# A two-layer hybrid trunk: low weight parts last in the feed-forward products, one product accumulated onto a copy in PSUM, forgetting attention in one visit per block

## The chip, the cores and the metric

The kernel runs on one core of a Trainium2 chip. The core has a matrix engine (TensorE, PE), which reads its stationary operand by separate weight loads (PEld in the profile), a vector engine (VectorE, DVE), a scalar engine (ScalarE, ACT), GpSimd (POOL) and SyncE (SP), which here only starts DMA transfers. Each engine works through its own list of instructions; semaphores tie the lists together. The metric is the device time of one execution in microseconds. Times below are from the profile of one execution unless they are called a median.

## The reference

Two layers over x of 512 x 1024 (float32). In each layer three head groups share one projection w_in: sliding-window attention (group A), forgetting attention (group B) and mLSTM (group C).

```python
h = _rms(x, norm1)
z = h @ w_in
...
x = x + jnp.concatenate([ya, yb, yc], axis=-1) @ w_out
u = _rms(x, norm2) @ w_ff1
return x + jnp.square(jax.nn.relu(u)) @ w_ff2
```

Group B, in blocks of 128 queries, is a causal softmax with a decay taken from cumulated log gates:

```python
s = jnp.einsum('bqhd,bkhd->bhqk', qi, k).astype(jnp.float32) / math.sqrt(D)
s = s + Fi[..., None] - FT[:, :, None, :]
...
p = jax.nn.softmax(s, axis=-1).astype(v.dtype)
return jnp.einsum('bhqk,bkhd->bqhd', p, v)
```

## The kernel before, in words

x lies transposed in SBUF (xT, eight tiles of 128 rows by 512 columns). Every weight arrives in tiles of 128 x 1024 float32 (512 KB). For each, ACT copies a rounded high part (`whi`, L203) and DVE subtracts it from the raw tile to get the low part (`wlo`, L204). There are three buffers of each, so the parts of three jobs exist at a time. A product of weights and activations is then three matmuls: high by high, high by low, low by high (`mm3`, L261 to L263).

Raw tiles lie in a ring of three (`raw0` to `raw2`), to which the feed-forward phase adds a ring of four (`fraw`). `load_part` issues the plain load on SP's queue (L156); where a tile is the sum of two blocks, the second block is added to it by an accumulating transfer issued on POOL's queue (L158). A load is issued when a tile of a ring has been given back, that is when its `whi` and `wlo` are made.

In the feed-forward phase (about 246 to 538 us and 776 to 1068 us of the span) two rounds of w1 go by the plain scheme. The other six, and w2, go by a scheme of seven products on 2 x 2 blocks in place of eight, in the order A11, S1, S2, A12, S4, S3, A22. Two of the seven weights are made on DVE from tiles that are there already: `prep_job` adds S1's tile into A11's for S2 (L214), and A12's into that for S4 (L218). S1 and S3 are sums that the accumulating transfer makes. So the addition at L214 needs two things: that A11's `whi` and `wlo` have been made, and that S1's accumulating transfer has landed.

`prod` runs one such product: 4 k-slices x 2 halves x 3 matmuls of 256 columns, 24 in all. `ff_pairs` interleaves them, one product of w2 (`ff2`), one of w1 (`ff1_st`). A round of 14 products is seven of each. After each product `acc` (L1265) adds the result into xT, or `ff1_st` copies, adds, takes relu and square (`act`), and splits the activations into high and low parts (`gsplit`, L1167 and L1168; `csplit`, L1172 and L1173). The order of each engine's list is not the order of the code: the framework's scheduler moves instructions of one engine past one another where the data allow it, so an edit in one place can move instructions elsewhere.

All eight PSUM banks (`at`) hand round between products. In `ff1_st` the first product's result X is copied to SBUF (`ct[:, 0]`, ACT), the A12 product goes to a fresh bank Y, and DVE adds the two (L1233).

In the attention phase a generator `big_work` yields pieces of the w_in and w_out products; `fill(us, stop)` pulls pieces until a credit is used up, so that PE has dense work between the small matmuls of the groups. `runB` makes blocks in three steps: `s1` (scores at L849, mask at L851, then maximum, exponential, scaling on DVE and ACT), `s2` (transposes at L874, copies) and `s3` (values, L891). Step i runs `s1(i)` and `s3(i-2)`, yields, runs `s2(i-1)`, and yields again. Its generator is advanced by the loops over group C, with `fill` between the visits.

Of the kernel before, what the change touches and what calls it, by code (L numbers as in the profile page):

```python
# [15 lines left out]
AF = mybir.ActivationFunctionType  # L16
ALU = mybir.AluOpType
AX = mybir.AxisListType

P = 128  # L20
# [30 lines left out]
def trunk(ctx, tc, x, cols, rows, gate_w, tabs, w_in, w_out, w1, w2, out):  # L51
    nc = tc.nc
    V, A, G, T = nc.vector, nc.scalar, nc.gpsimd, nc.tensor
# [38 lines left out]
    def smt(n, name):  # L92
        return sm.tile([P, n], F32, tag=f"sm{n}", name=nm(name))

    def v3(a, d=HD):
        return a.rearrange("p (h d) -> p h d", d=d)
# [163 lines left out]
    def mm3(o, sh, sl, mh, ml, first, last, skip=False):  # L260
        T.matmul(o, sh, mh, start=first, stop=False, skip_group_check=skip)  # L261
        T.matmul(o, sh, ml, start=False, stop=False, skip_group_check=skip)  # L262
        T.matmul(o, sl, mh, start=False, stop=last, skip_group_check=skip)  # L263
# [132 lines left out]
    def headrms(zt, nh, name):  # L396
        sq = wt("tmp", "hsq")
        A.activation(sq[:, :nh * HD], zt, AF.Square)
        ss = smt(nh, name)
        V.tensor_reduce(ss, v3(sq[:, :nh * HD]), AX.X, ALU.add)  # L400
        v = smt(nh, name + "v")
# [39 lines left out]
    FA, FB = 2.1, 0.33  # L441
    F0, F1, F2 = 0, 4.5, 1.5
    FG = 4
    for l in range(L):
# [77 lines left out]
        done = set()  # L522
# [64 lines left out]
        bw = big_work()  # L587
        credit = [0.0]

        def fill(us, stop=None):  # L590
            credit[0] += us
            while credit[0] > 0:
                if stop is not None and stop in done:
                    credit[0] = 0.0
                    return
                c = next(bw, None)
                if c is None:
                    credit[0] = 0.0
                    return
                credit[0] -= c  # L600

        def fill_to(mark):
            while mark not in done:
# [130 lines left out]
        def runA():  # L734
# [7 lines left out]
            def s1(c):  # L742
# [8 lines left out]
                for r in range(2):  # L751
                    V.tensor_reduce(v3(mx, 2)[:, :, r], v3(sc[r], 256)[:, :, :nk], AX.X, ALU.max)
                nmx = smt(4, "nmx")
# [83 lines left out]
        def runB(qTB, kTB):  # L837
            units = [(pr, n) for pr in range(2) for n in range(NT)]
            st, pobs, fbs = {}, {}, {}

            def s1(u):
                pr, n = units[u]
                if n == 0:
                    fbs[pr] = [rowb(gate["drow"], 2 * pr + r) for r in range(2)]
                nk = (n + 1) * P
                sps = [att(), att()]
                for r, sp in enumerate(sps):
                    rs = slice(r * 64, (r + 1) * 64)
                    T.matmul(sp[:, :nk], qTB[rs, pr, n * P:(n + 1) * P], kTB[rs, pr, :nk], start=True, stop=False)  # L849
                for sp in sps:  # L850
                    T.matmul(sp[:, n * P:nk], identb, trib, start=False, stop=True)  # L851
                scs = [wt("scs", "scs") for _ in range(2)]
                mx, nmx, ssum, rec = (smt(2, n_) for n_ in ("mxb", "nmxb", "ssb", "recb"))
                for r, sp in enumerate(sps):
                    V.tensor_tensor_reduce(scs[r][:, :nk], sp[:, :nk], fbs[pr][r][:, :nk], 1.0, -3.0e38, ALU.add,
                                           ALU.max, mx[:, r:r + 1])
                V.tensor_scalar(nmx, mx, -1.0, None, ALU.mult)
                for r in range(2):
                    A.activation(scs[r][:, :nk], scs[r][:, :nk], AF.Exp, bias=nmx[:, r:r + 1],
                                 accum_out=ssum[:, r:r + 1])  # L860
                V.reciprocal(rec, ssum)
                for r in range(2):
                    V.tensor_scalar(scs[r][:, :nk], scs[r][:, :nk], rec[:, r:r + 1], None, ALU.mult)
                st[u] = scs

            def s2(u):
                pr, n = units[u]
                nk = (n + 1) * P
                scs = st.pop(u)
                ps = []  # L870
                for r in range(2):
                    pt = att()
                    for b in range(n + 1):
                        T.transpose(pt[:, b * P:(b + 1) * P], scs[r][:, b * P:(b + 1) * P], ident)  # L874
                    p_ = wt("pT", "pTb")
                    if r:
                        A.activation(p_[:, :nk], pt[:, :nk], AF.Copy)
                    else:
                        V.tensor_copy(p_[:, :nk], pt[:, :nk])
                    ps.append(p_)  # L880
                st[u] = ps

            def s3(u):
                pr, n = units[u]
                if n == 0:
                    pobs[pr] = att()
                ps = st.pop(u)
                for b in range(n + 1):
                    for r in range(2):
                        h = 2 * pr + r  # L890
                        T.matmul(pobs[pr][r * 64:(r + 1) * 64, n * P:(n + 1) * P], zbv[b][:, h * 64:(h + 1) * 64],  # L891
                                 ps[r][:, b * P:(b + 1) * P], start=b == 0, stop=b == n)
                if n == NT - 1:
                    A.activation(yhi(4 + pr), pobs[pr], AF.Copy)
                    V.tensor_tensor(ylo(4 + pr), pobs[pr], yhi(4 + pr), ALU.subtract)

            for i in range(len(units) + 2):
                if i < len(units):
                    s1(i)
                if 0 <= i - 2 < len(units):  # L900
                    s3(i - 2)
                yield
                if 0 <= i - 1 < len(units):
                    s2(i - 1)
                yield
# [126 lines left out]
        bt = 0  # L1032
# [31 lines left out]
        cst_ = wt("qk", "state")[:, :780].rearrange("p (b r v) -> p b r v", b=3, r=2)  # L1064
        G.memset(cst_, 0.0)
        for i in range(8):
            if i % 2 == 0:
                next(gb)
            fill(FB, "wo0")
            if i % 2 == 1:  # L1070
                prepC(i // 2, kTC)
                if i // 2 < NT - 1:
                    stateC(i // 2, cst_)
        gc, c_tail = runC(qTC, kTC, cst_)
        ct, bt = 0, 0
        for _ in gc:
            ct += 1
            fill(FB, "wo0")
            if 5 * bt < 2 * ct:
                bt += 1  # L1080
                next(gb, None)
                fill(FB, "wo0")
        for _ in gb:
            fill(FB, "wo0")
        fill_to("wo0")
        c_tail(0)
        fill_to("wo1")
# [7 lines left out]
        ct = v3(wt("ct", "ct"), S)  # L1095
# [11 lines left out]
        def bank():  # L1107
            return banks.popleft()
# [16 lines left out]

        def prod(bk, bh, bl, start):
            ws = getjob()
            for kk in range(4):
                hi, lo = ws[kk]
                for f in range(2):  # L1130
                    c = slice(f * P, (f + 1) * P)
                    mm3(bk[:, f * 256:(f + 1) * 256], hi[:, c], lo[:, c], bh(kk), bl(kk), start and kk == 0 and f == 0,
                        kk == 3 and f == 1, True)

        def prod1(bk, op, start=True):
            bh, bl = xop(op, 0), xop(op, 1)
            prod(bk, lambda kk: bh[:, kk, :], lambda kk: bl[:, kk, :], start)
# [37 lines left out]
        def act(a, src, sign):  # L1175
            A.activation(ct[:, a], src, AF.Relu, scale=sign)
            A.activation(ct[:, a], ct[:, a], AF.Square)
# [39 lines left out]
                    yield  # L1217

        def ff1_st(s, rr):
            X = bank()  # L1220
            prod1(X, 0)
            A.activation(ct[:, 0], X, AF.Copy)
            yield
            Z = bank()
            prod1(Z, 3)
            A.activation(ct[:, 3], Z, AF.Copy)
            yield
            prod1(X, 4, False)
            A.activation(ct[:, 1], X, AF.Copy)
            yield  # L1230
            Y = bank()
            prod1(Y, 1)
            V.tensor_tensor(ct[:, 0], Y, ct[:, 0], ALU.add)  # L1233
            banks.append(Y)
            act(0, ct[:, 0], 1.0)
            csplit(s, rr)
            yield
            prod1(Z, 2, False)
            V.tensor_tensor(ct[:, 1], Z, ct[:, 1], ALU.add)
            banks.append(Z)  # L1240
            act(1, ct[:, 1], 1.0)
            n1_()
            yield
            prod1(X, 5, False)
            V.tensor_tensor(ct[:, 3], X, ct[:, 3], ALU.add)
            act(3, ct[:, 3], -1.0)
            n2_(s, rr)
            yield
            prod1(X, 6, False)
            act(2, X, -1.0)  # L1250
            banks.append(X)
            tail_(s, rr)
            yield
# [23 lines left out]
        def ff2(s):  # L1277
# [18 lines left out]
            for dg in range(2):  # L1296
                Y = bank()
                prod2(Y, s, 1)
                acc(s, dg, 0, 0, Y, True)
                banks.append(Y)  # L1300
# [102 lines left out]
```

## Time and profile before

| | |
|---|---|
| median of three runs | 1079.09 us (1073.43 to 1081.91) |
| profiled execution: time, span | 1074.93 us, 1073.2 us |
| granted TensorE clock | 0.997 |
| PE busy, matmuls | 1059.1 us, 8376 |
| weight loads busy | 989.8 us |
| DVE busy | 911.9 us |
| ACT busy | 626.4 us |
| POOL busy | 103.8 us |

In the lists of waits a row names who waited for whom, then the total in us, the number of times and the longest. In timeline rows stand the start, the length, engine, line, operation, output and inputs, and in brackets how long the engine idled before and for what. In the chain of waits in order of time a row is a start, a length and what took it. "at<-xhl,whi" is a product into a PSUM bank of an activation tile and a high weight part; the activation tiles are called xhl, xbx, yg and gx. A start of a matmul is measured, its end is modelled, so distances are taken from start to start.

### The profile page before, as it was taken

The numbers are of one execution on the slowest core, as the hardware profiler recorded it, in microseconds if no ns is written. First come the engines' busy times: TensorE is split into PE (matmuls) and PEld (weight loads), VectorE is DVE, ScalarE is ACT, GpSimd is POOL, SyncE is SP. The second block draws the span as 40 slices with busy tenths as digits, with TensorE's granted clock in tenths as the row PEclk, the third lists the DMA queues.
The fourth block names the chain that finished last, engine by engine and source line by source line (L and its number), as shares of the span: only waits on it lengthen the run. The fifth ranks groups of instructions, "written<-read, shape, count | busy, mean of one in ns | idle before, by whom it ended". The sixth has DMA issues, their size and how long they took to land.

```text
span 1073.2 us, 20903 instructions
## 1 busy us (share of the span) xinstructions
PE 1059.1 (99%) x8376; PEld 989.8 (92%) x8376; DVE 911.9 (85%) x1550; ACT 626.4 (58%) x1097; POOL 103.8 (10%) x154
## 2 busy tenths in 40 slices
PE   8999999999999999999999999999999999999998
PEld 8999977887999999999999998778789999999998
DVE  6696877899997997988977878688999889799897
ACT  5446655376666566566454567444765665576662
POOL 2030020101010010010001200101000100000100
PEclk8999999999999999999999999999999999999999
DMA  6533121145478588588435321213334866876872
GB/s 200 164 110 109 59 68 50 62 174 118 118 197 215 140 213 209 149 210 223 108 108 155 102 80 41 86 44 136 112 87 141 233 178 172 219 183 191 211 185 99
DMA packets 47346, 151.81 MB, mean 141 GB/s; under 512 B 5632, under 2 KB 8832, under 8 KB 47248
## 3 DMA queue, kind: packets, MB, share of 16 engines
q1 hardware_dynamic: 39184, 121.10, 33.8%
q0 software_dynamic: 8064, 29.36, 16.2%
q8 instruction: 66, 1.08, 0.4%
q14 instruction: 32, 0.26, 0.1%
HBM read 147.86 MB, written 2.13 MB: 140 GB/s over the span
## 4 chain that ended last, share of the span: by engine, by line
PE 80%; DVE 11%; ACT 3%; DMA 3%; issue 1%; SPq 0%; DVEq 0%; POOLq 0%
PE at L261 24%; PE at L263 24%; PE at L262 24%; DMA raw<-in_w_dram 3%; DVE wlo L204 2%; DVE rt L719 2%; PE at L849 1%; PE at L891 1%; PE at L874 1%; ACT whi L203 1%; ACT pe L762 1%; PE at L972 1%; DVE yg L1168 1%; DVE z L715 1%; DVE z L721 1%
## 5 line engine op out<-in xcount | busy, mean ns | idle before, releaser
L203 ACT ACTIVATE whi<-raw 128x1024 fp32r<-128x1024 f32 (+1 forms) x144 | 150.9, 1048 | 143.7 <-PE at L262 103.2
L204 DVE TENSOR_TENSOR wlo<-raw,whi 128x1024 fp32r<-128x1024 f32 (+1 forms) x144 | 173.8, 1207 | 41.2 <-ACT whi L203 40.7
L203 ACT ACTIVATE whi<-fraw 128x1024 fp32r<-128x1024 f32 x122 | 129.2, 1060 | 92.4 <-PE at L262 76.2
L261 PE MATMUL at<-yg,whi 128*128 128x256 f32 (+1 forms) x592 | 179.8, 307 | 0.0
L263 PE MATMUL at<-yg,wlo 128*128 128x256 f32 (+1 forms) x592 | 178.4, 301 | 0.0
L262 PE MATMUL at<-xhl,whi 128*128 128x256 f32 (+1 forms) x576 | 177.9, 309 | 0.0
L262 PE MATMUL at<-yg,whi 128*128 128x256 f32 (+1 forms) x560 | 169.6, 303 | 0.0
L261 PE MATMUL at<-whi,xhl 128*128 128x256 f32 (+1 forms) x576 | 164.1, 285 | 2.1 <-ACT whi L203 1.3
L262 PE MATMUL at<-wlo,xhl 128*128 128x256 f32 (+1 forms) x576 | 161.5, 280 | 0.3 <-DVE wlo L204 0.3
L263 PE MATMUL at<-whi,xhl 128*128 128x256 f32 (+1 forms) x576 | 161.5, 280 | 0.0
L261 PE MATMUL at<-xhl,whi 128*128 128x256 f32 (+1 forms) x512 | 161.1, 315 | 0.0
L263 PE MATMUL at<-xhl,wlo 128*128 128x256 f32 (+1 forms) x512 | 160.3, 313 | 0.0
L204 DVE TENSOR_TENSOR wlo<-fraw,whi 128x1024 fp32r<-128x1024 f32 x122 | 148.9, 1221 | 8.6 <-ACT whi L203 8.1
L261 PEld LDWEIGHTS at<-yg,whi 128*128 128x128 f32 x592 | 111.2, 188 | 5.6 <-issue 1.7
L263 PEld LDWEIGHTS at<-yg,wlo 128*128 128x128 f32 x592 | 111.2, 188 | 5.3
L262 PEld LDWEIGHTS at<-xhl,whi 128*128 128x128 f32 x576 | 108.0, 188 | 7.6 <-issue 0.5
L261 PEld LDWEIGHTS at<-whi,xhl 128*128 128x128 f32 x576 | 109.4, 190 | 3.2 <-ACT whi L203 1.6
L262 PEld LDWEIGHTS at<-wlo,xhl 128*128 128x128 f32 x576 | 109.5, 190 | 0.5 <-DVE wlo L204 0.5
L263 PE MATMUL at<-xbx,wlo 128*128 128x256 f32 x384 | 106.6, 278 | 3.4 <-DVE wlo L204 3.4
L263 PEld LDWEIGHTS at<-whi,xhl 128*128 128x128 f32 x576 | 109.3, 190 | 0.3 <-DVE xhl L328 0.3
L262 PEld LDWEIGHTS at<-yg,whi 128*128 128x128 f32 x560 | 105.3, 188 | 4.2 <-DVE yg L1002 0.5
L261 PE MATMUL at<-xbx,whi 128*128 128x256 f32 x384 | 106.1, 276 | 0.0
(286 smaller groups left out, 2423.1 us busy)
## 6 DMA issues: line engine op xcount, KB each, us to landing
fraw<-in_w_dram SPq DMA_DIRECT2D x90, 512.0 KB, 4.5
raw<-in_w_dram SPq DMA_DIRECT2D x66, 512.0 KB, 4.5
raw<-in_w_in_dram SPq DMA_DIRECT2D x34, 512.0 KB, 3.4
fraw<-in_w_dram POOLq DMA_DIRECT2D x34, 512.0 KB, 6.0
raw<-in_w_dram POOLq DMA_DIRECT2D x22, 512.0 KB, 7.9
raw<-in_w_out_dram SPq DMA_DIRECT2D x16, 512.0 KB, 3.4
rowb<-drow SPq DMA_DIRECT2D x16, 256.0 KB, 4.0
raw<-in_w_in_dram SPq DMA_DIRECT2D x12, 256.0 KB, 3.8
```

The lines of the kernel that those rows point to most:

```text
L203: A.activation(hi[:, cs_], raw[:, cs_], AF.Copy)
L204: V.tensor_tensor(lo[:, cs_], raw[:, cs_], hi[:, cs_], ALU.subtract)
L261: T.matmul(o, sh, mh, start=first, stop=False, skip_group_check=skip)
L262: T.matmul(o, sh, ml, start=False, stop=False, skip_group_check=skip)
L263: T.matmul(o, sl, mh, start=False, stop=last, skip_group_check=skip)
L715: V.tensor_tensor(z10, z10, bc(rq), ALU.mult)
L719: V.tensor_tensor(r10[:, oo:oo + n, a:a + 32], z10[:, oo:oo + n, b:b + 32], tb(S_, n, a, a + 32), ALU.mult)
L721: V.tensor_tensor(zaq[t], ro[:, :640], rt[:, :640], ALU.add)
L762: A.activation(pe[:, u, :nk], sc[u % 2][:, (u // 2) * 256:(u // 2) * 256 + nk], AF.Exp, bias=nmx[:, u:u + 1], accum_out=ssum[:, u:u + 1])
L849: T.matmul(sp[:, :nk], qTB[rs, pr, n * P:(n + 1) * P], kTB[rs, pr, :nk], start=True, stop=False)
L874: T.transpose(pt[:, b * P:(b + 1) * P], scs[r][:, b * P:(b + 1) * P], ident)
L891: T.matmul(pobs[pr][r * 64:(r + 1) * 64, n * P:(n + 1) * P], zbv[b][:, h * 64:(h + 1) * 64], ps[r][:, b * P:(b + 1) * P], start=b == 0, st ...
```

## The change

Three edits. First, `prod` (the seven-product scheme alone) issues the sixteen matmuls with the high weight part for all k-slices and halves, and then the eight with the low part. Second, in `ff1_st` the first product's result is copied by ACT into a second PSUM bank Y, the A12 product accumulates onto it, and relu reads Y; the addition at L1233 is gone. Third, `runB` does one visit per block in place of two, the driving loops advance it half as often, and `fill` takes the w_out pieces in pairs.

```diff
-        def fill(us, stop=None):
+        def fill(us, stop=None, n=1):
             credit[0] += us
             while credit[0] > 0:
-                if stop is not None and stop in done:
...
-                credit[0] -= c
+                for _ in range(n):
...
+                    credit[0] -= c
...
                 if 0 <= i - 2 < len(units):
                     s3(i - 2)
-                yield
                 if 0 <= i - 1 < len(units):
                     s2(i - 1)
                 yield
...
         for i in range(8):
-            if i % 2 == 0:
+            if i % 4 == 0:
                 next(gb)
-            fill(FB, "wo0")
+            fill(FB, "wo0", 2)
...
-            if 5 * bt < 2 * ct:
+            if 5 * bt < ct:
                 bt += 1
                 next(gb, None)
-                fill(FB, "wo0")
+                fill(2 * FB, "wo0", 2)
         for _ in gb:
-            fill(FB, "wo0")
+            fill(2 * FB, "wo0", 2)
...
         def prod(bk, bh, bl, start):
             ws = getjob()
-            for kk in range(4):
-                hi, lo = ws[kk]
-                for f in range(2):
-                    c = slice(f * P, (f + 1) * P)
-                    mm3(bk[:, f * 256:(f + 1) * 256], hi[:, c], lo[:, c], bh(kk), bl(kk), start and kk == 0 and f == 0,
-                        kk == 3 and f == 1, True)
+            for i in range(2):
+                for kk in range(4):
+                    for f in range(2):
+                        c, o = slice(f * P, (f + 1) * P), bk[:, f * 256:(f + 1) * 256]
+                        w = ws[kk][i][:, c]
+                        T.matmul(o, w, bh(kk), start=start and i == kk == f == 0, stop=i == 1 and kk == 3,
+                                 skip_group_check=True)
+                        if i == 0:
+                            T.matmul(o, w, bl(kk), start=False, stop=False, skip_group_check=True)
...
         def ff1_st(s, rr):
-            X = bank()
+            X, Y = bank(), bank()
             prod1(X, 0)
-            A.activation(ct[:, 0], X, AF.Copy)
+            A.activation(Y, X, AF.Copy)
             yield
...
-            Y = bank()
-            prod1(Y, 1)
-            V.tensor_tensor(ct[:, 0], Y, ct[:, 0], ALU.add)
+            prod1(Y, 1, False)
+            act(0, Y, 1.0)
             banks.append(Y)
-            act(0, ct[:, 0], 1.0)
             csplit(s, rr)
```

What PE runs in one FF1 product of layer 0 (the one with weights whi_631 and wlo_632; xhl is the activation, at_ the bank), the last rows before the change:

```order
L261 MATMUL at_546_2966<-xhl_90,whi_631_4167 128x256
L262 MATMUL at_546_2966<-xhl_90,whi_631_4167 128x256
L263 MATMUL at_546_2966<-xhl_90,wlo_632_4168 128x256
L261 MATMUL at_546_2966<-xhl_90,whi_631_4167 128x256
L262 MATMUL at_546_2966<-xhl_90,whi_631_4167 128x256
L263 MATMUL at_546_2966<-xhl_90,wlo_632_4168 128x256
```

and the same product after it:

```order
L1133 MATMUL at_547_2967<-xhl_90,whi_631_4165 128x256
L1136 MATMUL at_547_2967<-xhl_90,whi_631_4165 128x256
L1133 MATMUL at_547_2967<-xhl_90,whi_631_4165 128x256
L1136 MATMUL at_547_2967<-xhl_90,whi_631_4165 128x256
L1133 MATMUL at_547_2967<-xhl_90,wlo_632_4166 128x256 x8
```

The low part wlo_632 stood third of each three and is now read by the last eight alone.

DVE's list at the same place (342.6 to 355 us of the span before): wlo_630 is the low part of an A11 tile of w2, raw1_74 that tile's raw weights, raw2_75 those of S1. Before:

```order
L204 TENSOR_TENSOR wlo_630_4138<-raw1_74,whi_629_4137 128x1024
L1183 SCALAR_TENSOR_TENSOR ct_527_2865<-ct_527_2865 128x512
L1184 TENSOR_TENSOR ct_527_2865<-ct_527_2865 128x512
L1265 TENSOR_TENSOR xT_89<-xT_89,at_544_2964 128x2x256
L204 TENSOR_TENSOR wlo_632_4168<-fraw_528_2866,whi_631_4167 128x1024
L1168 TENSOR_TENSOR gx_526_2864<-ct_527_2865,gx_526_2864 128x1024
L214 TENSOR_TENSOR fraw_528_2866<-fraw_528_2866 128x1024
L204 TENSOR_TENSOR wlo_634_4203<-fraw_528_2866,whi_633_4202 128x1024
L214 TENSOR_TENSOR raw1_74<-raw2_75,raw1_74 128x1024
L1168 TENSOR_TENSOR yg_91<-ct_527_2865,yg_91 128x1024
```

and after, where the lines of `ff1_st` and `acc` have moved by one to three (L1183 is L1186, L1184 is L1187, L1168 is L1171, L1265 is L1266):

```order
L204 TENSOR_TENSOR wlo_630_4136<-raw1_74,whi_629_4135 128x1024
L214 TENSOR_TENSOR raw1_74<-raw2_75,raw1_74 128x1024
L1186 SCALAR_TENSOR_TENSOR ct_527_2865<-ct_527_2865 128x512
L1187 TENSOR_TENSOR ct_527_2865<-ct_527_2865 128x512
L1266 TENSOR_TENSOR xT_89<-xT_89,at_545_2965 128x2x256
L1171 TENSOR_TENSOR gx_526_2864<-ct_527_2865,gx_526_2864 128x1024
L204 TENSOR_TENSOR wlo_632_4166<-fraw_528_2866,whi_631_4165 128x1024
L204 TENSOR_TENSOR wlo_634_4201<-fraw_528_2866,whi_633_4200 128x1024
L1171 TENSOR_TENSOR yg_91<-ct_527_2865,yg_91 128x1024
L1266 TENSOR_TENSOR xT_89<-xT_89,at_544_2964 128x2x256
```

The addition of S1's tile into A11's (L214 on raw1_74) has moved from eight instructions behind wlo_630 to the place directly behind it, ahead of wlo_632 and wlo_634; the other L214 of this stretch, on fraw, now comes later. The same holds for the five other L214 additions of one raw tile into another. The lists of POOL are the same as before; in SP's, one pair of loads into different rings has changed places in each layer.

More of the change, by code (lines that the diff above doesn't have):

```diff
@@ L588, in trunk @@
         credit = [0.0]
-        def fill(us, stop=None):
+        def fill(us, stop=None, n=1):
             credit[0] += us
             while credit[0] > 0:
-                if stop is not None and stop in done:
[L594 to L599, printed above, removed]
-                credit[0] -= c
+                for _ in range(n):
+                    if stop is not None and stop in done:
+                        credit[0] = 0.0
+                        return
+                    c = next(bw, None)
+                    if c is None:
+                        credit[0] = 0.0
+                        return
+                    credit[0] -= c
         def fill_to(mark):
@@ L1077, in trunk @@
             ct += 1
-            fill(FB, "wo0")
-            if 5 * bt < 2 * ct:
+            fill(FB, "wo0", 2)
+            if 5 * bt < ct:
                 bt += 1
                 next(gb, None)
-                fill(FB, "wo0")
+                fill(2 * FB, "wo0", 2)
         for _ in gb:
-            fill(FB, "wo0")
+            fill(2 * FB, "wo0", 2)
         fill_to("wo0")
```

## The prediction

> **What bounds the kernel now.** I read the busy table and the chain of the profile's page first, then the list of waits, then the timeline around the longest of them.
>
> ```profile
> PE 1059.1 (99%) x8376; PEld 989.8 (92%) x8376; DVE 911.9 (85%) x1550; ACT 626.4 (58%) x1097; POOL 103.8 (10%) x154
> PE 80%; DVE 11%; ACT 3%; DMA 3%; issue 1%; SPq 0%; DVEq 0%; POOLq 0%
> PEld at L263 <- DVE wlo L204: 4.3, 5, 1.2
> PEld L851 <- issue: 6.5, 12, 0.8
> 316.00:354.00 38.00, 38.00 (x337) 38.00 (x337) 30.47 (x32) 23.93 (x29) 3.48 (x4) 1.00 0.79 212
> 354.00:392.00 38.00, 36.95 (x326) 36.75 (x325) 35.70 (x40) 23.52 (x29) 3.46 (x4) 1.00 0.60 160
> ```
>
> TensorE (PE) is busy for 99% of the span and carries 80% of the chain. It does not get shorter: 8376 matmuls before and after. What can move is its waits. The third row is the only large one that another engine causes: five waits of weight loads at L263 (the low part of a weight) for the subtraction at L204 that makes this low part, 4.3 us in all. The two windows (length; then PE, PEld, DVE, ACT and POOL busy, with counts) give the pace: 38.00/337 = 0.113 us a matmul, so a product of 24 matmuls takes 2.71 us. They also show VectorE (DVE) idle for some 7.5 us in one round of 14 products and 2.3 us in the next.
>
> One of the five waits, on DVE and then on its chain:
>
> ```profile
> 342.62 1.23 DVE L204 TENSOR_TENSOR wlo<-raw,whi 128x1024 fp32r<-128x1024 f32 x1 [0.29 <-ACT whi L203]
> 343.80 0.69 DVE L1183 SCALAR_TENSOR_TENSOR ct<-ct 128x512 f32<-128x512 f32 x1
> 344.41 0.68 DVE L1184 TENSOR_TENSOR ct<-ct 128x512 f32<-128x512 f32 x1
> 345.01 0.68 DVE L1265 TENSOR_TENSOR xT<-xT,at 128x512 f32<-128x512 f32 x1
> 345.61 1.22 DVE L204 TENSOR_TENSOR wlo<-fraw,whi 128x1024 fp32r<-128x1024 f32 x1
> 346.75 1.22 DVE L1168 TENSOR_TENSOR gx<-ct,gx 128x1024 fp32r<-128x1024 f32 x1
> 348.03 1.23 DVE L214 TENSOR_TENSOR fraw<-fraw 128x1024 f32<-128x1024 f32 x1
> 349.17 1.22 DVE L204 TENSOR_TENSOR wlo<-fraw,whi 128x1024 fp32r<-128x1024 f32 x1
> 351.73 1.23 DVE L214 TENSOR_TENSOR raw<-raw,raw 128x1024 f32<-128x1024 f32 x1 [1.33 <-DMA raw<-in_w_dram]
> ...
> 355.20 1.22 DVE L204 TENSOR_TENSOR wlo<-fraw,whi 128x1024 fp32r<-128x1024 f32 x1
> ```
>
> ```profile
> 336.04 4.39 DMA raw<-in_w_dram
> 341.02 10.68 DMA raw<-in_w_dram
> 418.50 10.67 DMA raw<-in_w_dram
> ```
>
> ```profile
> 349.60 0.28 PE L261 MATMUL at<-xhl,whi 128*128 128x256 f32 x1
> ```
>
> DVE takes its instructions in turn. At 350.4 it comes to the S2 addition (L214, raw<-raw,raw), which needs the accumulating transfer that was issued at 341.02 and lands 10.68 us later, at 351.7. Everything behind it starts late, and the low part that PE wants 0.23 us into a product is there only at 355.20 + 1.22 = 356.42.
>
> **The change, part by part.**
>
> *Low parts last.* In the 7-product scheme a low part is wanted after 16 matmuls and not after two: 16 x 0.113 = 1.81 us into the product in place of 0.23. The longest of the five waits was 1.2, less than the 1.58 us gained. With DVE's order unchanged all 4.3 us would go: -4.3. Matmuls and weight loads stay as many. The high part's buffer also comes free 8 matmuls (0.9 us) before the product ends, so the next split, and with it the release of the raw weights and the next load, can come up to 0.9 us sooner.
>
> *DVE's order does change.* In the rows of the order, the S2 addition into raw1 now stands directly behind the split of wlo_630 and ahead of five instructions it used to follow: the two ct operations, the accumulation into xT, the split's gx, and wlo_632. Its input is not ready sooner by more than those 0.9 us, since the transfer hangs on plain load, accumulation and ring, none of which moved. DVE reaches it at 343.80, when wlo_630 is done. It then waits until 351.73 - 0.9 = 350.8: 7.0 us idle in place of 1.33. Behind it come, by start-to-start distances in the rows above, the addition (1.14), three of 0.6, the gx split (1.14), and then wlo_632 (1.22): 5.3 us, ready at 356.1. Its product starts at 349.60 and wants it at 349.60 + 1.80 = 351.4. PE stalls 4.7 us, or 5.6 if nothing of the 0.9 is realised.
>
> The order shows the same move at all six such additions. This is what they have in the trace:
>
> ```profile
> L214 DVE TENSOR_TENSOR raw<-raw,raw 128x1024 f32<-128x1024 f32 x6 | 7.3, 1222 | 3.6 <-DMA raw<-in_w_dram 3.6
> 498.76 0.69 DVE L1183 SCALAR_TENSOR_TENSOR ct<-ct 128x512 f32<-128x512 f32 x1
> 487.15 0.86 POOL L158 DMA_DIRECT2D raw<-in_w_dram  x1 [8.77 <-DMA raw<-in_w_dram]
> 873.34 0.69 DVE L1183 SCALAR_TENSOR_TENSOR ct<-ct 128x512 f32<-128x512 f32 x1
> 869.41 0.89 POOL L158 DMA_DIRECT2D raw<-in_w_dram  x1 [2.10 <-DMA raw<-in_w_dram]
> raw<-in_w_dram POOLq DMA_DIRECT2D x1, 512.0 KB, 8.0
> 950.15 0.69 DVE L1183 SCALAR_TENSOR_TENSOR ct<-ct 128x512 f32<-128x512 f32 x1
> 957.48 1.23 DVE L214 TENSOR_TENSOR raw<-raw,raw 128x1024 f32<-128x1024 f32 x1 [0.90 <-DMA raw<-in_w_dram]
> 1027.06 0.69 DVE L1183 SCALAR_TENSOR_TENSOR ct<-ct 128x512 f32<-128x512 f32 x1
> 1015.61 0.89 POOL L158 DMA_DIRECT2D raw<-in_w_dram  x1 [8.98 <-DMA raw<-in_w_dram]
> ```
>
> L1183 starts where the addition will now stand, so its start is the moment at which DVE arrives; at the first place that is 343.80, 7.93 us before the data.
> - Second place: issued at 418.50, again 10.67 us, the whole pattern 77.5 us on. The same 4.7 (5.6).
> - Third: issued at 487.15; even 10.7 us later is 497.8, before DVE arrives at 498.76. Nothing.
> - Fourth: issued at 869.41, and the row behind it, of this one transfer, gives 8.0: landed at 877.4, 4.07 us after 873.34. That is 3.86 less than at the first place: 0.8 (1.7).
> - Fifth: DVE arrives at 950.15, data at 957.48: 7.33, or 0.6 less than the first: 4.1 (5.0).
> - Sixth: 1015.61 + 10.7 = 1026.3, before 1027.06. Nothing.
>
> Sum: 4.7 + 4.7 + 0.8 + 4.1 = 14.3 us, 17.9 without the 0.9. I take 14.3, because the list of waits has the splits on ScalarE (ACT) held by PE's release of the high part, which is what now comes sooner:
>
> ```profile
> ACT whi L203 <- PE at L262: 179.4, 140, 4.2
> ```
>
> A rule of the Trainium skill speaks for a far shorter transfer. In "DMA: Bandwidth & Descriptors", section "Anatomy of one DMA — SWDGE (gpsimd) path", a transfer issued from GpSimd is fitted as about 2.0 us and its bytes at 436 GB/s, which for 512 KB is an estimate of 3.2 us. The trace does not agree: 10.68, 10.67 and 8.0 us from issue to landing. By the page the data would be there at 344.2, no new stall would arise, and the sum would be -4.3.
>
> *A12 onto a copy in PSUM.* Twelve additions leave DVE, and one copy per round (ACT) now writes a PSUM bank:
>
> ```profile
> L1233 DVE TENSOR_TENSOR ct<-at,ct 128x512 f32<-128x512 f32 x12 | 8.3, 691 | 3.6 <-PE at L263 3.5
> L1222 ACT ACTIVATE ct<-at 128x512 f32<-128x512 f32 x12 | 6.9, 578 | 0.0
> ```
>
> These 8.3 us lie beside PE, so their removal by itself is worth nothing; it helps DVE win back what it loses at the additions. No row shows ACT writing PSUM. The copy of 0.58 us could be longer or shorter, and I take 0.58: the next product to touch the bank comes after five others, 5 x 2.71 = 13.6 us later, so even 2 us more would be hidden. The bank itself is taken three FF1 products sooner than before; by a count of takes and releases one of the eight is still free then, so PE does not wait for it. 0.
>
> *Forgetting attention in one visit.* The same matmuls in another order among the w_out pieces:
>
> ```profile
> 150.00:202.00 52.00, 52.00 (x358) 39.07 (x357) 41.99 (x140) 25.34 (x74) 6.90 (x18) 1.00 0.15 47
> 160.07 0.50 PE L261 MATMUL at<-yg,whi 128*128 128x512 f32 x1
> 160.41 0.39 PE L262 MATMUL at<-yg,whi 128*128 128x512 f32 x1
> 157.40 0.40 PE L263 MATMUL at<-yg,wlo 128*128 128x512 f32 x1
> 157.63 0.40 PE L261 MATMUL at<-yg,whi 128*128 128x512 f32 x1
> ```
>
> PE shows no idle time there. A change of tile shape costs 0.34 - 0.23 = 0.11 us (first matmul after L891 against a plain pair). The order has as many changes of shape as before, so at best one is cheaper in some eight of the visits: -0.9. At worst one block in each layer waits for its copies by the longest wait above, 0.8: +1.6. I take 0, the middle being near it.
>
> **Sum.** -4.3 + 14.3 + 0 + 0 = +10.0 us, with own bounds of +9 (the attention's gain) and +15 (no 0.9, the attention's loss). The profiled execution took 1074.93 us (span 1073.2), so it would become 1084.9. The median of the three runs, 1079.09, lies 4.2 above the profiled one; I predict for the median: 1079.1 + 10.0 = 1089.1, own range 1088 to 1094.
>
> **Rivals.**
> - *DVE does not win it back* (slower still). After such a wait the next item at risk is the S2 sum of the FF1 product four products on. From the start of the late addition it is the ninth of the 1.14 us instructions with five of 0.6: 13.3 us, with ACT's 1.06 split 14.4; PE gets there 5.3 + 0.9 + 3 x 2.71 = 14.3 us after the same start. The margin is nil. If of the two fraw additions that now stand together the other comes first, 1.75 us are added at the three large places, 5.3; without the 0.9 another 3.6. Total 10.0 + 8.9 = +18.9: 1098. It decides as soon as DVE is later than that margin. For: DVE busy 35.70 of 38 us in the round that follows. Against: 2.3 us of idle time there, and 0.69 us a round less work.
> - *The transfer is there in time* (not slower). If the landing comes 5 us sooner, the addition costs nothing wherever it stands, and only the first term is left: -4.3, so 1074.8. For: accumulating transfers into the other ring have a median of 6.0, and those into this one 7.9. Against: the three places that count have 10.68 and 10.67, and at 957.48 again data that come after DVE. It decides below some 6 us from issue to landing; each us above costs about 1 us at three places.
>
> ```profile
> fraw<-in_w_dram POOLq DMA_DIRECT2D x34, 512.0 KB, 6.0
> raw<-in_w_dram POOLq DMA_DIRECT2D x22, 512.0 KB, 7.9
> ```
>
> By the Trainium skill's fit above this second rival would be the rule; the trace is against it with every one of these rows.
>
> **How the numbers follow.** A measurement of this kernel can tell about 1%, 10.8 us, from no change. My forecast gets 0.65, DVE that stays late 0.15, the transfer in time 0.15, anything else 0.05. The forecast's +9 to +15 lies on both sides of the 1% line, its likeliest value just inside: of its 0.65 some 0.37 are within, 0.28 above. Slower by over 1%: 0.28 + 0.15 = 0.43 and 0.01 of the rest, 0.44. Within 1%: 0.37 and 0.14 of the second rival, 0.51. Faster by over 1% needs more than any term here gives: the last 0.01 of that rival and 0.04 of the rest, 0.05. The range reaches from the second rival's neighbourhood to the first's: 1075 to 1099.
>
> **What would show it.** In the changed kernel's profile the group L214 raw<-raw,raw should show some 20 to 25 us of idle time before it, caused by DMA, in place of 3.6: about 7 at three of its six rows, about 3 at one, none at two. Weight loads of low parts should wait for the subtraction about four times, 4 to 5 us each at three places, at matmul 17 of a product; the waits of 0.8 and 1.2 us should be gone. ACT's copy into PSUM should take about 0.6, and the attention stretches should stay without idle time on PE. I am wrong if DVE shows no idle time there, if PE's waits are much below DVE's less 2.5 us, or if PE waits for high parts too.

## The result, and the profile after

Six executions of the changed kernel have a median of 1091.87 us (1088.13 to 1095.56); six of the kernel before on the same chip 1078.84 us (1072.12 to 1081.91). The ratio is 1.013, with a 95% interval of 1.0087 to 1.0174: the change makes the kernel slower by some 13 us. Ratios, here and below, leave out executions more than 1.5% above the fastest of their kernel and are not exactly the quotients of the medians. The profiled execution took 1094.22 us, its span is 1092.4.

The busy table and the chain of the page, then one row of the list of waits, then two rows of the groups by line:

```profile
PE 1069.4 (98%) x8376; PEld 1002.0 (92%) x8376; DVE 901.5 (83%) x1538; ACT 624.2 (57%) x1097; POOL 101.4 (9%) x154
PE 71%; DVE 15%; DMA 7%; ACT 3%; issue 3%; SPq 0%; DVEq 0%; ACTq 0%; POOLq 0%
PEld at L1133 <- DVE wlo L204: 11.1, 4, 4.8
L214 DVE TENSOR_TENSOR raw<-raw,raw 128x1024 f32<-128x1024 f32 x6 | 7.4, 1226 | 22.1 <-DMA raw<-in_w_dram 22.1
L1225 ACT ACTIVATE at<-at 128x512 f32<-128x512 f32 x12 | 7.0, 580 | 0.0
```

PE has the same 8376 matmuls and DVE twelve instructions fewer. DMA's share of the chain has gone from 3% to 7%, DVE's from 11% to 15%. The six S2 additions had 3.6 us of idle time in front of them and now have 22.1, all of it waiting for the raw tile's transfer. PE's weight loads of low parts waited five times for 4.3 us and now wait four times for 11.1.

At the first place, DVE's timeline and PE's (the row of 350.88 is the last high part of that product, the next one the first low part), and the four transfers in the chain of waits in order of time:

```profile
341.83 1.22 DVE L204 TENSOR_TENSOR wlo<-raw,whi 128x1024 fp32r<-128x1024 f32 x1
348.75 1.23 DVE L214 TENSOR_TENSOR raw<-raw,raw 128x1024 f32<-128x1024 f32 x1 [5.71 <-DMA raw<-in_w_dram]
...
351.70 1.23 DVE L1171 TENSOR_TENSOR gx<-ct,gx 128x1024 fp32r<-128x1024 f32 x1
352.84 2.35 DVE L204 TENSOR_TENSOR wlo<-fraw,whi 128x1024 fp32r<-128x1024 f32 x2
```

```profile
350.88 0.28 PE L1136 MATMUL at<-xhl,whi 128*128 128x256 f32 x1
354.12 1.06 PE L1133 MATMUL at<-xhl,wlo 128*128 128x256 f32 x7 [2.96 <-DVE wlo L204]
```

```profile
338.77 9.89 DMA raw<-in_w_dram
420.48 8.99 DMA raw<-in_w_dram
877.71 10.40 DMA raw<-in_w_dram
962.26 8.49 DMA raw<-in_w_dram
```

DVE comes to the addition at 343.0 and stands until 348.75. From the addition to the start of the next low part it is 4.09 us, and PE loses 3.24 - 0.11 = 3.1 us at the change from high to low parts. At the other three places the distances from matmul to matmul are 1.95, 4.86 and 1.37 us.

That is not all of the loss. The windows of the same profile (length; PE busy with its count; the third number from the end is the granted clock) give another pace in some stretches:

```profile
270.30:350.80 80.50, 80.50 (x712) 80.50 (x711) 65.09 (x71) 48.72 (x60) 6.90 (x8) 1.00 0.68 184
363.50:432.90 69.40, 69.40 (x591) 69.40 (x591) 54.69 (x60) 40.72 (x50) 6.91 (x8) 1.00 0.77 204
898.40:974.70 76.30, 76.30 (x650) 76.30 (x649) 60.13 (x64) 42.96 (x53) 6.92 (x8) 1.00 0.73 193
893.95:898.05 4.10, 4.10 (x21) 4.10 (x21) 4.10 (x6) 3.28 (x5) 0.00 (x0) 0.50 0.01 2
```

80.50/712 is 113 ns a matmul, as before the change; 69.40/591 and 76.30/650 are 117.4, with no instruction of another kind in between and a granted clock of 1.00. The last row is the stretch behind the longest wait: 4.10/21 is 195 ns a matmul (213 from start to start, since the 21st only begins in the window), and here the granted clock is 0.50. The profile of before has one stretch at the slow pace inside its feed-forward phases:

```profile
936.80:961.90 25.10, 25.10 (x214) 25.10 (x214) 22.54 (x26) 17.30 (x21) 2.62 (x3) 1.00 0.75 189
```

The first two slow stretches of the changed kernel do not begin at a wait of the lists. At the first, ACT has waited for DVE's addition of an S2 sum on `fraw`, makes its high part, and PE starts the product that reads it, the fourth behind the one that stood:

```profile
362.17 2.01 ACT L203 ACTIVATE whi<-fraw 128x1024 fp32r<-128x1024 f32 x2 [3.05 <-DVE fraw L214]
363.29 0.38 PE L1133 MATMUL at<-xbx,whi 128*128 128x256 f32 x1
363.50 0.28 PE L1136 MATMUL at<-xbx,whi 128*128 128x256 f32 x1
```

The row of ACT is two splits; the first is done at 363.23, the weight load behind it comes 0.1 us late, and the second matmul starts 0.21 us after the first in place of 0.113. From there on the distances are 117.8 ns. The same stands at 444.14 (0.19 us), where the next slow stretch begins, and at 985.41 (0.21 us), behind which the pace stays at 113.3.

### The profile page after: what moved, and what is told of

It reads as the page before. It is cut to its first block, busy times and chain, and to the rows that moved or that the text cites. A ratio compares the mean times of both kernels' runs of the same rounds, so it can differ in the third digit from the quotient of the medians.

```text
span 1092.4 us, 20901 instructions
## 1 busy us (share of the span) xinstructions
PE 1069.4 (98%) x8376; PEld 1002.0 (92%) x8376; DVE 901.5 (83%) x1538; ACT 624.2 (57%) x1097; POOL 101.4 (9%) x154
## 4 chain that ended last, share of the span: by engine, by line
PE 71%; DVE 15%; DMA 7%; ACT 3%; issue 3%; SPq 0%; DVEq 0%; ACTq 0%; POOLq 0%
PE at L1133 24%; PE at L1136 12%; PE at L261 10%; PE at L262 9%; PE at L263 9%; DMA raw<-in_w_dram 6%; DVE wlo L204 4%; DVE rt L720 2%; PE at L750 1%; PE at L892 1%; DVE xT L1266 1%; PE at L875 1%; ACT whi L203 1%; DVE raw L214 1%; DVE z L716 1%
## 5 line engine op out<-in xcount | busy, mean ns | idle before, releaser
L1133 PE MATMUL at<-yg,whi 128*128 128x256 f32 x464 | 111.6, 279 | 0.2 <-ACT whi L203 0.2
L1136 PE MATMUL at<-yg,whi 128*128 128x256 f32 x432 | 104.0, 279 | 0.0
L1136 PE MATMUL at<-xhl,whi 128*128 128x256 f32 x416 | 99.9, 280 | 0.0
L1133 PE MATMUL at<-xbx,whi 128*128 128x256 f32 x384 | 91.3, 279 | 0.5 <-DVE ct L1246 0.5
L1136 PE MATMUL at<-xbx,whi 128*128 128x256 f32 x384 | 90.9, 278 | 0.0
L1266 DVE TENSOR_TENSOR xT<-xT,at 128x512 f32<-128x512 f32 x112 | 76.3, 681 | 15.5 <-PE at L1133 15.0
L1133 PE MATMUL at<-gx,whi 128*128 128x256 f32 x368 | 88.6, 278 | 0.0
L1133 PEld LDWEIGHTS at<-yg,whi 128*128 128x128 f32 x464 | 87.8, 189 | 0.4 <-ACT whi L203 0.4
L1133 PE MATMUL at<-xhl,whi 128*128 128x256 f32 x352 | 84.5, 280 | 0.0
L1136 PEld LDWEIGHTS at<-yg,whi 128*128 128x128 f32 x432 | 81.8, 189 | 0.0
L1136 PE MATMUL at<-gx,whi 128*128 128x256 f32 x336 | 80.9, 278 | 0.0
L1136 PEld LDWEIGHTS at<-xhl,whi 128*128 128x128 f32 x416 | 78.9, 190 | 0.0
```

Source lines behind the costliest of these rows:

```text
L1133: T.matmul(o, w, bh(kk), start=start and i == kk == f == 0, stop=i == 1 and kk == 3, skip_group_check=True)
L1136: T.matmul(o, w, bl(kk), start=False, stop=False, skip_group_check=True)
L1266: V.tensor_tensor(t_, t_, q2(bk), ALU.subtract if i else ALU.add)
```

## The experiments

The theory: with low parts last, the scheduler puts DVE's S2 addition ahead of other work, where DVE stands until the accumulating transfer lands, and PE stands for the low parts behind it. Rivals: one of the other two edits, or PE's own new order.

**The changed kernel again, and low parts last alone.** The second is the kernel before with the new `prod` and nothing else.

> The changed kernel once more, with the kernel before on the same chip, as the reference for the other runs. The theory (DVE waits at the S2 additions, PE waits behind it) expects +9 to +15 us over before, idle time of 20 to 25 us before the group L214 raw<-raw,raw, and waits of PE for low parts of 10 us or more. A rival (the loss is in a slower pace of the matmuls, 118 ns from start to start in some stretches, and not in waits) expects these stretches at the same places and as long as in the first profile, about 200 us of them.

> The low parts last, alone: A12's addition on DVE and forgetting attention as before. In its order DVE's S2 additions stand where the whole change has them, directly behind A11's low part. The theory expects nearly all of the loss, +8 to +15 us, with 20 us or more of idle time before L214 raw<-raw,raw. The rivals (the copy in PSUM or the attention's order costs the time) expect -4 us, the waits that go.

Measured: 1089.51 us (1.0142, interval 1.0084 to 1.02) and 1094.0 us (1.0184, 1.0142 to 1.0226). The addition's group and PE's wait, first in the repeated kernel, then in the one with low parts last alone:

```profile
L214 DVE TENSOR_TENSOR raw<-raw,raw 128x1024 f32<-128x1024 f32 x6 | 7.4, 1226 | 24.5 <-DMA raw<-in_w_dram 24.4
PEld at L1133 <- DVE wlo L204: 14.2, 4, 4.6
```

```profile
L214 DVE TENSOR_TENSOR raw<-raw,raw 128x1024 f32<-128x1024 f32 x6 | 7.4, 1226 | 25.9 <-DMA raw<-in_w_dram 25.8
PEld at L1133 <- DVE wlo L204: 15.2, 4, 4.2
```

The first edit alone carries the whole loss; the intervals of the two overlap (both against the kernel before on one chip, median 1073.92 us). The repeat settles one rival of the reading above: its profile has almost no stretch at 117.8 ns in the feed-forward phases, and yet the loss and the waits. So the slow pace is not needed for the loss; it comes and goes, and in the first profile it was a good part of it.

**The additions put back.** The whole change, with an order-only dependency for the six additions (it also goes to the other S2 additions, which did not stand in the way; `lo_ins` is the subtraction that makes a job's low part):

```diff
-            V.tensor_tensor(a, g["S1"]["raw"], a, ALU.add)
+            at = next(i for i, j in enumerate(jobs) if j is g["A11"]) + 2
+            with tc.issue_after(jobs[at]["lo_ins"].ins):
+                V.tensor_tensor(a, g["S1"]["raw"], a, ALU.add)
```

> The whole change, but each S2 addition of one raw tile into another is kept on DVE behind the low part two products after A11's (the wlo_634 of the first place), where it stood before the change. The theory expects the loss to vanish: -4 us against before, 13 to 18 under the changed kernel, idle time before L214 (here L216) back to a few us, and no wait of PE for low parts over 0.5 us. The rival that PE's own order or the other edits cost the time expects +9 to +15, as the changed kernel.

and later still, behind the low part of S1's own tile:

```diff
-            V.tensor_tensor(a, g["S1"]["raw"], a, ALU.add)
+            with tc.issue_after(g["S1"]["lo_ins"].ins):
+                V.tensor_tensor(a, g["S1"]["raw"], a, ALU.add)
```

> The whole change with each S2 addition kept behind the low part of its own S1 tile, later than before the change; by then the data has landed for that low part anyway. The theory expects no idle time of DVE for DMA at the additions at all and -4 to -5 us against before. What could spoil it: S1's raw tile is given back some 10 us later, so the next load into it starts later; if that ring is tight, PE waits for high parts appear and it is slower than the run with the additions in the old place.

Measured: 1076.69 us (1.0007, 0.9971 to 1.0043) in the old place, and 1069.24 us (0.9948, 0.9922 to 0.9974) behind S1's low part. The additions' groups in the two:

```profile
L216 DVE TENSOR_TENSOR raw<-raw,raw 128x1024 f32<-128x1024 f32 x6 | 7.3, 1223 | 3.5 <-DMA raw<-in_w_dram 3.5
```

```profile
L215 DVE TENSOR_TENSOR raw<-raw,raw 128x1024 f32<-128x1024 f32 x6 | 7.3, 1220 | 0.0
```

The loss hangs on the place of the additions and on nothing else that the change does. In the old place I had expected -4 and got no difference; six of its twelve executions lie at 1070.5 to 1073.3, the others at 1080 to 1082 and at 1091. The profile, of one of the fastest (1071.2), has one wait of 0.8 us left in each feed-forward phase, for a high part:

```profile
PEld at L1135 <- ACT whi L203: 1.6, 2, 0.8
```

The kernel with late additions has no such wait, and its twelve executions lie between 1068.21 and 1070.29. What I feared for it, the ring of raw tiles, does not show.

**The transfer taken away, the order left.** S1 is loaded by its first block alone; the accumulating transfer of its second block is left out.

```diff
-        for ap in jb["ap"][1:]:
+        for ap in jb["ap"][1:1 if jb["which"] == "S1" else None]:
```

> The whole change, but S1's tile is loaded by the plain transfer alone: the accumulating transfer that adds its second block is left out. DVE's order is that of the changed kernel, row for row at the S2 additions. The theory (DVE waits there for the landing of the accumulating transfer) expects the idle time before L214 raw<-raw,raw to fall from 22 us to under 3, no wait of PE for low parts over 1 us, and -4 to -6 us against before. The rival that the order itself is bad, whatever the transfer does, expects +5 us or more.

Measured: 1069.9 us (0.993, 0.9901 to 0.9959).

```profile
L214 DVE TENSOR_TENSOR raw<-raw,raw 128x1024 f32<-128x1024 f32 x6 | 7.4, 1226 | 0.2
```

With the additions in the early place and their data there, DVE does not wait at them, and the loss is gone. The early place costs only what the accumulating transfer is late. (This run also takes transfers off POOL's queue; the kernel with late additions keeps them all, and gains as much.)

**The other two edits without the first.**

> The two other edits without the low parts last: the products by threes as before, A12 onto the copy in PSUM and forgetting attention in one visit. DVE's S2 additions stand where they stood before the change. The theory expects no loss: within 3 us of before, the waits of PE for low parts still there (about 4 us). A rival in which one of these edits costs a third of the loss expects +4 us or more.

Measured: 1079.1 us (1.002, 0.9982 to 1.0057). PE's waits for low parts are the old ones, three caught here:

```profile
PEld at L263 <- DVE wlo L204: 2.9, 3, 1.2
```

Together they are worth nothing that can be measured.

**Does a short wait set the slow pace off?** The kernel with late additions has none of it in its feed-forward phases. Into it goes, ahead of each FF1 round, a small product, four small ACT copies and a second small product that reads the copy; the control reads the constant. An order-only dependency, not shown in the cut, keeps the first large matmul behind them. In both, the small products use the bank of the copy, and the output is another one; the large matmuls are the same.

```diff
             X, Y = bank(), bank()
+            T.matmul(Y[:, :64], ones_m, ones_m[:, :64], start=True, stop=True)
+            A.activation(stt, Y[:, :64], AF.Copy)
+            for _ in range(3):
+                A.activation(stt, stt, AF.Copy)
+            hold["ins"] = T.matmul(Y[:, 64:128], ones_m, stt[:, :64], start=True, stop=True)
             prod1(X, 0)
```

> The changed kernel with the S2 additions late (which had no stall in the feed-forward phase and ran within 2 us of itself), and with one short wait of PE put in front of each of the twelve FF1 rounds of the seven-product scheme: a small product, four small copies on ACT, and a second small product that reads the copy. Two readings of the slow stretches (118 ns in place of 113 from matmul to matmul) are told apart. If a stall can tip the pace of the matmuls into the slower rhythm until the next stall, stretches of 118 ns should begin or end at these waits, and the time should lie above the control run by more than the waits alone (some 10 us), with a spread of 5 us or more between executions. If the slow stretches have nothing to do with stalls, it is the control plus the waits, and as steady as that.

> The control of the run before: the same small products and copies, but the second small product reads the constant, so nothing waits. Both readings expect the time of the kernel with late additions plus some 2 us (24 more small products), no stall in the feed-forward phase, few or no stretches at 118 ns there, and a spread of about 2 us.

Measured: 1089.39 us (1.0123, 1.0083 to 1.0163), executions from 1087.82 to 1095.65; the control 1092.84 us (1.016, 1.0115 to 1.0205), from 1088.42 to 1098.38. The control is no control: its second product still waits for the first copy to have read the bank. The waits of the two, the one with the wait first:

```profile
PEld at L1236 <- ACT stt L1235: 4.7, 12, 0.5
```

```profile
PEld at L1236 <- ACT stt L1233: 3.1, 12, 0.3
```

Both waits are far under what I had meant to put in, and both kernels lose 20 us and more on the kernel with late additions (1069.24, on another chip). About 10 us of that is the small products themselves, for which I had expected 2. The second feed-forward phase from its first to its last matmul, in the control, where all but the first few matmuls behind its first small product run at the fast pace, and in the kernel with late additions:

```profile
809.70:1081.40 271.70, 271.04 (x2377) 269.83 (x2375) 235.15 (x252) 167.47 (x216) 21.65 (x25) 1.00 0.65 177
```

```profile
796.90:1063.30 266.40, 266.40 (x2352) 266.40 (x2351) 234.81 (x252) 161.84 (x192) 21.64 (x25) 1.00 0.67 180
```

That is 5.3 us for six rounds. The rest is in the pace. Four stretches between the small products of the first kernel, then two of the control:

```profile
276.50:311.80 35.30, 35.30 (x302) 35.30 (x301) 32.49 (x36) 22.34 (x28) 3.43 (x4) 1.00 0.60 168
314.10:350.80 36.70, 36.70 (x326) 36.70 (x325) 28.64 (x31) 23.25 (x29) 3.47 (x4) 1.00 0.81 214
353.30:390.00 36.70, 36.70 (x326) 36.70 (x326) 33.04 (x34) 23.42 (x29) 3.45 (x4) 1.00 0.58 165
392.40:430.60 38.20, 38.20 (x326) 38.20 (x326) 28.97 (x32) 23.65 (x29) 3.46 (x4) 1.00 0.78 208
```

```profile
275.00:311.90 36.90, 36.90 (x316) 36.90 (x314) 34.31 (x37) 23.53 (x32) 3.43 (x4) 1.00 0.58 162
816.10:851.20 35.10, 35.10 (x312) 35.10 (x311) 33.53 (x36) 22.86 (x32) 2.74 (x4) 1.00 0.60 174
```

35.30/302 is 116.9, the next two are 112.6, then 117.2; in the control 116.8 and 112.5. From start to start each stretch holds one pace, 117.8 or 113.3 ns, from its first products to its last, and the changes lie at the small products. The control was in the slow pace through the whole first feed-forward phase, from its first small product on, and in the fast one through the second, but for 19 matmuls at its start. So the first reading holds in its main point: an interruption of PE can tip the pace until another interruption. I had expected the control to be free of it, and it was not; nor did the kernel with the longer wait lie above the control.

**What is the first edit worth without the early additions?** The kernel before with late additions, and the kernel before with low parts last and late additions.

> The kernel before with one edit: each S2 addition of one raw tile into another is kept on DVE behind the low part of its S1 tile. The products are by threes, as before. If low parts last have a worth of their own, the waits at the first rounds (0.8 us each, at about 278 and 808 us) stay here, and with them the chance of the slow pace behind them: single executions at about 1070, 1080 and 1090 us. If the late additions alone make the gain, it is as steady as the changed kernel with late additions, 1068 to 1071 us in all executions.

> Low parts last and the S2 additions late, without the copy in PSUM and without the change in forgetting attention. If the other two edits are worth nothing, it runs like the whole change with late additions: 1069 to 1071 us in every execution, no stall and one pace, 113 ns, through each feed-forward phase. If the twelve additions that the copy in PSUM takes from DVE are needed to keep the low parts in time, waits for low parts show up, and with them slower executions.

Measured: 1079.85 us (1.0006, 0.9973 to 1.0039) and 1068.51 us (0.9916, 0.9888 to 0.9943), with the kernel before at 1079.73 on this chip. The sorted executions, in us:

```
before_late   1071.98 1072.28 1072.66 1073.03 1073.90 1079.64 1080.05 1080.08 1080.18 1080.50 1080.74 1081.00
lo_late       1067.94 1067.99 1068.04 1068.29 1068.36 1068.48 1068.54 1068.55 1068.84 1069.40 1069.71 1071.21
add_mid       1070.49 1070.86 1071.20 1071.34 1073.07 1073.29 1080.10 1081.54 1081.96 1090.84 1091.33 1091.39
```

Late additions alone do not help: short waits of PE are left, if not where I had expected them (0.2 to 0.5 us at the first rounds, 0.7 at the last), and with them two groups of times. With low parts last as well there is none, and each feed-forward phase is one stretch at the fast pace:

```profile
269.00:532.60 263.60, 263.60 (x2327) 263.60 (x2326) 237.64 (x259) 165.12 (x198) 21.61 (x25) 1.00 0.67 181
795.00:1061.30 266.30, 266.30 (x2351) 266.30 (x2350) 237.64 (x258) 161.20 (x192) 21.64 (x25) 1.00 0.67 181
```

This kernel beats both. The copy in PSUM and the one visit, which the kernel with late additions has besides, add nothing to it: 1069.24 and 1068.51, each on its own chip.

## Why the prediction was right or wrong

I forecast 1089.1 us for the median, own range 1088 to 1094, and 1091.9 came; the mechanism on which the forecast stood is shown by the runs, but by the first profile the waits alone would not have brought the time into the range. By its steps:

- *DVE's order.* Right. The additions in the early place cost the time (0.9948 and 1.0142, on one chip, differ by the place of the S2 additions alone), and only because the data are late (0.993 with the transfer left out).
- *The four places.* I had DVE wait some 7 us at three of the six, 3 at one and not at two, 20 to 25 in all. It was 5.71, 4.80, 7.33 and 4.23, nothing at two, 22.1 in all. The sizes of the single ones were off because the transfers are not constant: at the first place the plain load took 3.27 us where the trace of before had 4.39, and the accumulation 9.89 in place of 10.68; at the fourth place it took 10.40 where I had carried over 8.0. The chain behind the addition was right (4.08 us by the distances that I gave, 4.09 measured).
- *PE's waits.* I summed 14.3 us; the three profiles with the early additions show 11.1, 14.2 and 15.2. The sum is of the right size, the places are not: 4.7, 4.7, 0.8 and 4.1 were forecast, and in the first profile it was 3.1, 1.8, 4.7 and 1.3. That the errors partly cancel in the sum is luck. What held at each place is the step from DVE to PE, DVE's wait less some 2.5 to 3 us.
- *The old waits, -4.3.* They went: no wait of a low part at the first rounds is left in the changed kernel.
- *The copy in PSUM and the attention, 0.* Right: 1.002 (0.9982 to 1.0057) together. The copy took 580 ns, as from PSUM to SBUF.
- *The sum.* It has two holes, and here the step that failed is "-4.3 + 14.3 + 0 + 0": it prices a wait of PE at its length. In the first profile the span grew by 19.2 us. The waits account for 11.1 - 4.3 = 6.8. The matmuls behind the longest one ran at half the clock, 20 of them at 213 ns in place of 113: 2.0 us. And 590, some 890 and 649 matmuls in three stretches ran at 117.8 in place of 113.3, 9.5 us, where the profile of before had 214 such in its feed-forward phases, 1.0 us. Two new waits near the end (0.6 us at 1045.3 for an addition on DVE, 0.3 at 1062.3 for a high part) and the three of 0.1 make 1.3. That is 18.6 of 19.2; the rest I have not traced. In the repeated profile the slow stretches are all but absent and the half clock takes more (50 matmuls), so these two parts differ from one execution to the next. That the forecast came within 3 us is in part luck: with the waits alone, 6.8 us on the 1078.84 of before, it would have been 1085.6, under my range, and the profiled execution, for which I had 1084.9, took 1094.22.
- *The rivals.* DVE won its delay back, but for the margin that I had called nil: PE waited 0.1 us for the S2 sum four products on, at three of the four places. One of my signs of being wrong, a wait of PE for high parts, so did show. As a wait it costs next to nothing, but two of the three slow stretches begin there. That the transfer would be there in time was the rival for which I had cited "DMA: Bandwidth & Descriptors" in the Trainium skill, section "Anatomy of one DMA — SWDGE (gpsimd) path", with an estimate of 3.2 us for 512 KB. The four accumulating transfers behind which DVE stood took 8.49 to 10.40 us here.
- *The chances.* I put 0.44 on slower by over 1% and 0.51 on less; the ratio of 1.013, with its interval from 0.9% on, is on the slower side. The two missing terms are what I had too little of.

## What to carry to other kernels

An edit that only reorders matmuls can move instructions on another engine; compare the order of every engine, and for each instruction that has moved ahead ask whether its data come from a transfer and when, by the trace, that lands. An instruction that waits for a transfer belongs behind the last one that does not need it, and where a scheduler thinks otherwise, an order-only dependency is enough (here from 1.4% slower to 0.5% faster). And in a kernel bound by PE, count the interruptions of its stream as well as their length: the versions without any in the feed-forward phases were the fastest and the steadiest.

## What the runs showed of the hardware

Two things that I had not expected.

First, the stream of back-to-back matmuls with 256 columns, each with its own weight load, has two paces, 113.3 and 117.8 ns from start to start, at a granted clock of 1.00. A stretch keeps its pace: 2351 matmuls at 113.3 in the fastest kernel, 649 at 117.8 between two waits of the changed one. The changes that I looked at in the feed-forward phases lie at an interruption, such as a wait of 0.1 us (213 ns from one matmul to the next at 363.29 in the changed kernel) or a small product of another kind, or at the edge of the phase. Not every interruption changes the pace, and which of the two follows differs between executions. A feed-forward phase of 2330 matmuls in the slow pace costs 2330 x 4.5 ns = 10.5 us, and the groups of execution times above lie some 7.5 us (the kernel before with late additions) and 10 us apart (the additions in the old place). That the pace explains these groups is argued from this: there is a profile of one execution of each kernel only. DVE's and ACT's instructions take as long in the slow stretches as in the fast ones. What in the array or the weight loads makes the difference stays open.

Second, a long wait is followed by half the clock. Of PE's waits for low parts in three profiles (the changed kernel twice, low parts last alone), given as the distance from matmul to matmul, those of 2.75 us and less were followed by none, one of 3.24 by none, those of 3.21 and 3.27 by 15 matmuls at 213 ns each, and all six from 3.89 to 4.86 by 12 to 20. The half clock began at once or up to 1.7 us after the wait's end. A window behind the one of 3.27 in the repeated kernel, with its granted clock:

```profile
433.60:436.50 2.90, 2.90 (x15) 2.90 (x15) 2.90 (x5) 2.08 (x3) 0.00 (x0) 0.50 0.00 0
```

The Trainium skill has this rule in "TensorE: Matmul & The Clock Gate", section "HAM oscillation — how this bites in real kernels": no idle gaps of PE above about 3.4 us. The trace agrees to within 0.3 us: the idle time is the distance less 0.11, and eight of the nine gaps of 3.1 us and more were followed by half the clock, none of the shorter ones. I had priced the waits of 4.7 us without it.
